# A four-layer encoder step on one core: score matrices of two heads issued in turn, and PSUM banks dealt out anew

## The chip, the core and the metric

The kernel runs on one core of a Trainium2 chip. That core has a matrix engine (TensorE, PE in the profile, with its weight loads as PEld), a vector engine (VectorE, DVE), an activation engine (ScalarE, ACT), a general engine (GpSimd, POOL) and a queue that issues DMAs (SP). Matrix results go to PSUM, which the kernel uses as eight banks of 128 partitions by 512 floats; everything else lies in SBUF. The metric is device time in microseconds (us) of one launch, the median of three runs.

## What is computed

One step of a streaming encoder: 512 prompt rows and 128 sample rows (8 groups of 16) of width 1024 go through two layers. Layer 0 has stick-breaking attention (8 heads of 64) beside a gated linear recurrence, layer 1 has chunk-band softmax attention (16 heads of 64); each layer ends in a gated feed-forward network of 2816. The sample rows also attend to 512 cached keys and values per group. Cut to what the change touches:

```python
def _sb_block(q, k, v, q_pos, k_pos):            # layer 0
    z = einsum('bthd,bshd->bhts', q, k) * HEAD_DIM ** -0.5
    mask = k_pos[None, :] < q_pos[:, None]
    log_beta = log_sigmoid(z)
    log_keep = where(mask, log_sigmoid(-z), 0.0)
    rev = cumsum(log_keep, axis=3, reverse=True)
    w = where(mask, exp(log_beta + after), 0.0)  # after: rev moved on by one
    return einsum('bhts,bshd->bthd', w, v)

def _band_attn(q, k, v, q_pos, k_pos, rel_table): # layer 1
    s = einsum('bthd,bshd->bhts', q, k) * HEAD_DIM ** -0.5
    s = s + rel_table[:, rel]
    p = softmax(where(mask, s, -inf))
    return einsum('bhts,bshd->bthd', p, v)
```

## The kernel before, in words

The program is a chain of stages: the stick-breaking layer (0 to 447 us of the profile), its feed-forward network, the chunk-band layer (about 885 to 1369 us), the second feed-forward network. Large products are made of two rounded halves of each operand, so that three matmuls stand for one.

**Prompt attention** (`attend_prompt`, L426) takes heads in pairs and, for each pair, four blocks of 128 query rows against n = 128, 256, 384 and 512 keys. A head has 64 channels, so head 0 of a pair lies in partitions 0 to 63 of `qT` and `kT` and head 1 in 64 to 127, and the three score matmuls of a head (L436, L437, L438) use 64 rows of the matrix engine. Before, one head's three matmuls are written together, its scores `z` become weights on the vector and activation engines (`stick_break` L400, `softmax` L413), the weights are transposed back into the same bank `z` (L444), copied out (L447 on ACT for head 0, L449 on DVE for head 1), and the result of both heads goes into the first head's bank (L455) and out at L457. So one bank is held from the first score to the end of its block.

**Sample attention** (`attend_sample`, L473) runs for each of 8 groups, once in the stick-breaking layer and twice (two halves of the heads) in the chunk-band layer, so 8 and 16 samples. A sample loads 1 MB of values (`vr`, L481) and four key tiles of 256 KB (`kr`, four buffers, L486). Each key tile is transposed on the matrix engine (`kttp`, L489), copied to SBUF (`kt`, two buffers: L494 on ACT, L492 on DVE) and gives a quarter of the scores (`zs`, L496). The scores are copied out (L499), become weights, are transposed (L508), copied (L509); the weights of the new keys are transposed (L510) and copied (L511); then come the products with the values (L517), a copy (L520), a last transpose (L521) and two copies to `oS` (L525). Before, all the PSUM results of a sample after the key tiles use the sample's score bank `zs`.

**PSUM.** Three banks (`pps`) serve the projections. The other five are two pools inside `mixer_pools`: before, 3 banks `za` and 2 banks `zb` in the stick-breaking layer, 4 and 1 in the chunk-band layer. `za` held scores; `zb` held the recurrence's results (`b_mix`), the transposed keys of the projections (`ktp`, L388) and key tiles. In the chunk-band layer (`KTC`) key tiles alternated between `zb` and `za`. Tiles of a pool take its banks in the order in which the program asks for them, so a tile that is asked for early and used late stands ahead of the later ones.

**What sets the order.** The program text gives each instruction a priority, and a scheduler of the framework fixes one order for each engine when the program is built; on the chip each engine works through its list in that order, and an instruction that waits holds up those behind it. Projections (`pw`, L288 to L290, and `pm`) and the output projection (`po`, L561 to L563) are the work that the scheduler puts between the steps of attention.

Of the kernel before, what the change touches and what calls it, by code (L numbers as in the profile page):

```python
# [16 lines left out]
P = 128  # L17
# [29 lines left out]
BANKS = ((3, 2), (4, 1))  # L47
KTA = "bbbb"
KTC = "baba"
# [6 lines left out]
def kernel(  # L56
# [8 lines left out]
    nc = tc.nc  # L65
# [360 lines left out]
    def attend_prompt(qT, kT, v, c0, odst, weights, mask):  # L426


        for b in range(4):
            n = (b + 1) * P  # L430
            bs = slice(b * P, n)
            wTs, zs = [], []
            for h in range(2):
                z = za([P, 512], "z")
                r = slice(64 * h, 64 * h + 64)
                MM(z[:, :n], lhsT=qT[r, 0, bs], rhs=kT[r, 0, :n], start=True, stop=False)  # L436
                MM(z[:, :n], lhsT=qT[r, 0, bs], rhs=kT[r, 1, :n], start=False, stop=False)  # L437
                MM(z[:, :n], lhsT=qT[r, 1, bs], rhs=kT[r, 0, :n], start=False, stop=not mask)  # L438
                if mask:
                    MM(z[:, bs], lhsT=identb, rhs=mask_a, start=False, stop=True)  # L440
                w = weights(h, n, z[:, :n])
                wT = vr_([P, b + 1, P], "wT")
                for j in range(b + 1):
                    nc.tensor.transpose(z[:, j * P:(j + 1) * P], w[:, j * P:(j + 1) * P], ident)  # L444
                zv = z[:, :n].rearrange("p (j t) -> p j t", t=P)
                if h == 0:
                    nc.scalar.copy(wT, zv)  # L447
                else:
                    nc.vector.tensor_copy(wT, zv)  # L449
                wTs.append(wT)  # L450
                zs.append(z)
            o = zs[0][:, :P]
# [20 lines left out]
    def attend_sample(ck, cv, b, cs, qbd, zn, vnew, weights, oS, kttp):  # L473
# [9 lines left out]
        for j in range(4):  # L483
# [3 lines left out]
            tp = (zb if kttp[j] == "b" else za)([P, 4, P], "kttp")  # L487
# [13 lines left out]
        w = weights(zs)  # L501
        wn = w5([P, DB, DS], "wn")
# [249 lines left out]
    stack.enter_context(mixer_pools(*BANKS[0]))  # L752
# [60 lines left out]
    def a_sample():  # L813
        with priority(FIRST + 100000):
            zn = new_key_scores(qbd, kfs, msn)
        for b in range(DB):
            with priority(FIRST + 100000 + 1000 * (b + 1)):
                attend_sample(cache_a_k, cache_a_v, b, slice(0, 512), qbd, zn, vt4[:, :512],
                              lambda zs: stick_break(528, zs, zs), oS[:, :4, :], KTA)
# [227 lines left out]

    stack.enter_context(mixer_pools(*BANKS[1]))
    W = w_qkv_c[0]
# [32 lines left out]
    def c_sample(half):  # L1082
# [11 lines left out]
        for b in range(DB):  # L1094
            with priority(p + 1000 * (b + 1)):
                attend_sample(cache_c_k, cache_c_v, b, cs, qbd[half], zn, vt4[:, cs],
                              lambda zs: softmax(528, zs, zs, bsam[:, ::-1]),
                              oS[:, 4 * half:4 * half + 4, :], KTC)
# [69 lines left out]
```

## Time and profile before

| | us |
|---|---|
| median of three runs (1822.29 to 1827.14) | 1823.97 |
| the profiled execution's own time | 1823.8 |
| its span in the trace | 1822.1 |
| TensorE busy (95% of the span) | 1732.9 |
| VectorE, ScalarE, GpSimd busy | 1142.8, 833.8, 327.7 |

In the page, a group of instructions has its line, its engine, its output and inputs by tile name, the shape and the count. Durations of matmuls run from the start of the read to a modelled end, so a matmul's duration is longer than the distance to the next one's start; where the argument is about throughput it uses distances of starts in the timeline. A matmul with f32 inputs stands as two in the trace, one with rounded inputs (the scores, projections) as one.

### The profile page before, as it was taken

The page shows a single profiled execution, that of the slowest core. Times are in us where ns is not written, and L with a number is a line of the kernel's source. Part 1 is how long each engine was busy: PE and PEld are TensorE (multiplying, and loading weights), DVE is VectorE, ACT ScalarE, POOL GpSimd, SP SyncE. Part 2 cuts the span into 40 slices and gives each one's busy share as a digit, 9 for nine tenths or more (in the row PEclk, how much of TensorE's full clock was granted, in tenths as well). Part 3 has the DMA queues.
Part 4 walks back from the last instruction along what each step waited for, and adds up shares of the span by engine and source line. Part 5 has one row for each costly group of instructions (what it writes and reads, how often), then busy time and mean ns, then how long its engine had stood idle before and what let it go on. Part 6 is the DMA issues. An engine that isn't in the chain of part 4 may idle for free.

```text
span 1822.1 us, 31879 instructions
## 1 busy us (share of the span) xinstructions
PE 1732.9 (95%) x12504; PEld 1550.1 (85%) x12504; DVE 1142.8 (63%) x2285; ACT 833.8 (46%) x1837; POOL 327.7 (18%) x355
## 2 busy tenths in 40 slices
PE   8999998998899999999799999999878999999997
PEld 7898986976898989989698888888757989999896
DVE  5466576767964846747635554665658747658475
ACT  6453444556642534525424333444545525435253
POOL 2000000002513413222200000000104314133130
PEclk9998997998999999999799999999988999999999
DMA  5311222573222232221342223257862222312212
GB/s 141 94 56 47 66 83 95 179 255 105 70 93 70 75 100 63 100 74 66 110 128 77 80 89 95 85 178 263 278 214 65 81 81 72 103 58 93 93 59 81
DMA packets 157430, 192.10 MB, mean 105 GB/s; under 512 B 13232, under 2 KB 109504, under 8 KB 157280
## 3 DMA queue, kind: packets, MB, share of 16 engines
q1 hardware_dynamic: 153696, 178.40, 30.4%
q0 software_dynamic: 3584, 11.67, 2.0%
q8 instruction: 98, 1.61, 0.4%
q14 instruction: 52, 0.43, 0.1%
HBM read 175.75 MB, written 14.29 MB: 104 GB/s over the span
## 4 chain that ended last, share of the span: by engine, by line
PE 80%; DVE 12%; DMA 4%; ACT 2%; issue 2%; SPq 0%; DVEq 0%; ACTq 0%
PE pn L307 6%; PE pn L309 5%; PE pn L308 5%; PE pw L288 5%; PE pw L289 5%; PE pw L290 5%; DVE wl L274 4%; PE px L653 3%; PE px L654 3%; PE px L655 3%; PE z L455 3%; PE py L655 3%; DMA kr<-in_cache_c_k_dram 2%; PE pm L337 2%; PE py L653 2%; PE py L654 2%
## 5 line engine op out<-in xcount | busy, mean ns | idle before, releaser
L274 DVE TENSOR_TENSOR wl<-raw,wh 128x512 fp32r<-128x512 f32 (+1 forms) x350 | 279.3, 807 | 220.8 <-ACT wh L273 218.7
L273 ACT CAST wh<-raw 128x512 fp32r<-128x512 f32 (+1 forms) x350 | 215.4, 618 | 347.3 <-PE pn L309 162.6
L659 POOL TENSOR_TENSOR sw<-raw 128x512 f32<-128x512 f32 x88 | 121.6, 1386 | 498.9 <-DMA raw<-in_w_ffn_gate_dram 292.9
L273 ACT CAST wh<-sw 128x512 fp32r<-128x512 f32 x176 | 109.3, 621 | 177.8 <-PE px L654 78.2
L274 DVE TENSOR_TENSOR wl<-sw,wh 128x512 fp32r<-128x512 f32 x176 | 139.7, 798 | 60.3 <-ACT wh L273 49.1
L308 PE MATMUL pn<-wl,gT 128*128 128x512 f32 x440 | 172.7, 393 | 0.0
L309 PE MATMUL pn<-wh,gT 128*128 128x512 f32 x440 | 170.7, 392 | 0.0
L307 PE MATMUL pn<-wh,gT 128*128 128x512 f32 x440 | 168.8, 394 | 0.0
L655 PE MATMUL py<-xb,wl 128*128 128x320 f32 x352 | 113.1, 321 | 8.4 <-DVE wl L274 8.2
L653 PE MATMUL py<-xb,wh 128*128 128x320 f32 x352 | 111.4, 316 | 6.1 <-ACT wh L273 4.6
L654 PE MATMUL pq<-xt,wh 128*128 128x320 f32 x352 | 109.1, 310 | 2.9 <-DVE xt L613 2.7
L654 PE MATMUL px<-xt,wh 128*128 128x320 f32 x352 | 109.7, 312 | 1.6 <-DVE xt L613 1.6
L654 PE MATMUL py<-xb,wh 128*128 128x320 f32 x352 | 110.7, 314 | 0.0
L653 PE MATMUL px<-xt,wh 128*128 128x320 f32 x352 | 109.5, 311 | 0.0
L655 PE MATMUL px<-xt,wl 128*128 128x320 f32 x352 | 109.4, 311 | 0.0
L653 PE MATMUL pq<-xt,wh 128*128 128x320 f32 x352 | 109.1, 310 | 0.1
L655 PE MATMUL pq<-xt,wl 128*128 128x320 f32 x352 | 108.6, 309 | 0.0
L309 PEld LDWEIGHTS pn<-wh,gT 128*128 128x128 f32 x440 | 83.5, 190 | 17.4
L308 PEld LDWEIGHTS pn<-wl,gT 128*128 128x128 f32 x440 | 83.6, 190 | 17.2
L307 PEld LDWEIGHTS pn<-wh,gT 128*128 128x128 f32 x440 | 83.4, 190 | 16.8
L288 PE MATMUL pw<-hTa,wh 128*128 128x320 f32 (+1 forms) x272 | 89.5, 329 | 0.0
L290 PE MATMUL pw<-hTa,wl 128*128 128x320 f32 (+1 forms) x272 | 88.7, 326 | 0.0
(331 smaller groups left out, 4778.3 us busy)
## 6 DMA issues: line engine op xcount, KB each, us to landing
raw<-in_w_ffn_gate_dram SPq DMA_DIRECT2D x44, 512.0 KB, 4.1
raw<-in_w_ffn_up_dram SPq DMA_DIRECT2D x44, 512.0 KB, 3.7
raw<-in_w_ffn_down_dram SPq DMA_DIRECT2D x44, 512.0 KB, 3.3
kr<-in_cache_c_k_dram SPq DMA_DIRECT2D x64, 256.0 KB, 4.8
vr<-in_cache_c_v_dram SPq DMA_DIRECT2D x16, 1024.0 KB, 6.7
raw<-in_w_in_ab_dram SPq DMA_DIRECT2D x24, 512.0 KB, 3.8
raw<-in_w_qkv_c_dram SPq DMA_DIRECT2D x24, 512.0 KB, 3.8
vr<-in_cache_a_v_dram SPq DMA_DIRECT2D x8, 1024.0 KB, 5.5
```

The lines of the kernel that those rows point to most:

```text
L273: nc.scalar.copy(H, rawv)
L274: nc.vector.tensor_sub(L, rawv, H.bitcast(F32))
L288: MM(ps[i], lhsT=H[:, k % 4, :], rhs=hT[k][:, 0, s], start=(k == 0), stop=False)
L289: MM(ps[i], lhsT=H[:, k % 4, :], rhs=hT[k][:, 1, s], start=False, stop=False)
L290: MM(ps[i], lhsT=L[:, k % 4, :], rhs=hT[k][:, 0, s], start=False, stop=(k == 7))
L307: MM(ps[b], lhsT=lhs[k][:, 0, bs], rhs=H, start=(k == 0), stop=False)
L308: MM(ps[b], lhsT=lhs[k][:, 0, bs], rhs=L, start=False, stop=False)
L309: MM(ps[b], lhsT=lhs[k][:, 1, bs], rhs=H, start=False, stop=(k == K - 1))
L653: MM(ps, lhsT=H[:, k, :], rhs=X[x][0][k], start=(first and k == 0), stop=False, **f)
L654: MM(ps, lhsT=H[:, k, :], rhs=X[x][1][k], start=False, stop=False, **f)
L655: MM(ps, lhsT=L[:, k, :], rhs=X[x][0][k], start=False, stop=(k == 3), **f)
L659: nc.gpsimd.tensor_tensor(t, a, b, op=op)
```

## The change

In `attend_prompt` both heads' score banks are asked for first, and the three score matmuls are written for head 0 and head 1 in turn. A score bank now ends with the weights: the transposes go to a tile `wtp` of `zb`, and the result into the first head's `wtp`. In `attend_sample` the score bank `zs` ends with the copy L499 (L502 after); all later PSUM results of the sample go to a new tile `zw` of `zb`, asked for after the weights. Every key tile is in `zb`. Both layers have 2 banks `za` and 3 banks `zb`; `ktp` and the recurrence share those three.

```diff
--- before.py
+++ after.py
@@ -44,9 +44,7 @@
 ORDER = "V0 P0 G0 P1 K0 V1 M0 P2 K1 R0 M1 R2 P3 R1 R3"
 MPRI = 50000
 WHEN = ((20, 20, 20, 20), (4, 8, 12, 15))
-BANKS = ((3, 2), (4, 1))
-KTA = "bbbb"
-KTC = "baba"
+BANKS = (2, 3)
 GROUPS = (6, 6, 6, 4)
 FIRST = -1000000
 LOGSET = "natural_log_exp_and_others"
@@ -426,30 +424,35 @@
     def attend_prompt(qT, kT, v, c0, odst, weights, mask):
 
 
+
         for b in range(4):
             n = (b + 1) * P
             bs = slice(b * P, n)
-            wTs, zs = [], []
-            for h in range(2):
-                z = za([P, 512], "z")
-                r = slice(64 * h, 64 * h + 64)
-                MM(z[:, :n], lhsT=qT[r, 0, bs], rhs=kT[r, 0, :n], start=True, stop=False)
-                MM(z[:, :n], lhsT=qT[r, 0, bs], rhs=kT[r, 1, :n], start=False, stop=False)
-                MM(z[:, :n], lhsT=qT[r, 1, bs], rhs=kT[r, 0, :n], start=False, stop=not mask)
-                if mask:
+            zs = [za([P, 512], "z") for _ in range(2)]
+
+            for i, j in ((0, 0), (0, 1), (1, 0)):
+                for h in range(2):
+                    r = slice(64 * h, 64 * h + 64)
+                    MM(zs[h][:, :n], lhsT=qT[r, i, bs], rhs=kT[r, j, :n], start=(i + j == 0),
+                       stop=(i == 1 and not mask))
+            if mask:
+                for z in zs:
                     MM(z[:, bs], lhsT=identb, rhs=mask_a, start=False, stop=True)
-                w = weights(h, n, z[:, :n])
+            ws_ = [weights(h, n, zs[h][:, :n]) for h in range(2)]
+            wTs, ts = [], []
+            for h, w in enumerate(ws_):
+                t = zb([P, 512], "wtp")
                 wT = vr_([P, b + 1, P], "wT")
                 for j in range(b + 1):
-                    nc.tensor.transpose(z[:, j * P:(j + 1) * P], w[:, j * P:(j + 1) * P], ident)
-                zv = z[:, :n].rearrange("p (j t) -> p j t", t=P)
+                    nc.tensor.transpose(t[:, j * P:(j + 1) * P], w[:, j * P:(j + 1) * P], ident)
+                tv = t[:, :n].rearrange("p (j t) -> p j t", t=P)
                 if h == 0:
-                    nc.scalar.copy(wT, zv)
+                    nc.scalar.copy(wT, tv)
                 else:
-                    nc.vector.tensor_copy(wT, zv)
+                    nc.vector.tensor_copy(wT, tv)
                 wTs.append(wT)
-                zs.append(z)
-            o = zs[0][:, :P]
+                ts.append(t)
+            o = ts[0][:, :P]
             for j in range(b + 1):
                 for h in range(2):
                     MM(o[64 * h:64 * h + 64, :], lhsT=v[:, j, c0 + 64 * h:c0 + 64 * h + 64],
@@ -470,7 +473,7 @@
             nc.vector.tensor_tensor(zn, zp, mask.unsqueeze(1).to_broadcast([P, DB, DS]), op=ALU.add)
         return zn
 
-    def attend_sample(ck, cv, b, cs, qbd, zn, vnew, weights, oS, kttp):
+    def attend_sample(ck, cv, b, cs, qbd, zn, vnew, weights, oS):
 
 
         def rows(src):
@@ -484,7 +487,7 @@
             kr = kr_([P, 512], "kr")
             with plain():
                 nc.sync.dma_start(kr, rows(ck)[:, j, :])
-            tp = (zb if kttp[j] == "b" else za)([P, 4, P], "kttp")
+            tp = zb([P, 4, P], "kttp")
             for p in range(4):
                 nc.tensor.transpose(tp[:, p, :], kr[:, p * P:(p + 1) * P], ident)
             kt = kt_([P, 4, P], "kt")
@@ -499,6 +502,7 @@
         nc.scalar.copy(zs[:, :512], z)
         nc.gpsimd.tensor_copy(zs[:, 512:], zn[:, b, :])
         w = weights(zs)
+        z = zb([P, 512], "zw")
         wn = w5([P, DB, DS], "wn")
         nc.gpsimd.memset(wn, 0.0)
         nc.gpsimd.tensor_copy(wn[:, b, :], w[:, 512:528])
@@ -749,7 +753,7 @@
 
 
     stack = ExitStack()
-    stack.enter_context(mixer_pools(*BANKS[0]))
+    stack.enter_context(mixer_pools(*BANKS))
     nc.scalar.preload_act_table_set(LOGSET)
     with priority(2 * FIRST):
         x0 = [load_x(x_rows(x_prompt, xs_flat, 0), 0)]
@@ -816,7 +820,7 @@
         for b in range(DB):
             with priority(FIRST + 100000 + 1000 * (b + 1)):
                 attend_sample(cache_a_k, cache_a_v, b, slice(0, 512), qbd, zn, vt4[:, :512],
-                              lambda zs: stick_break(528, zs, zs), oS[:, :4, :], KTA)
+                              lambda zs: stick_break(528, zs, zs), oS[:, :4, :])
 
 
     def b_gates():
@@ -1045,7 +1049,7 @@
     hT = hT2
 
 
-    stack.enter_context(mixer_pools(*BANKS[1]))
+    stack.enter_context(mixer_pools(*BANKS))
     W = w_qkv_c[0]
     vt4 = v4([P, D], "vt4c")
     vc = [vp([P, 4, 512], "vc") for _ in range(2)]
@@ -1095,7 +1099,7 @@
             with priority(p + 1000 * (b + 1)):
                 attend_sample(cache_c_k, cache_c_v, b, cs, qbd[half], zn, vt4[:, cs],
                               lambda zs: softmax(528, zs, zs, bsam[:, ::-1]),
-                              oS[:, 4 * half:4 * half + 4, :], KTC)
+                              oS[:, 4 * half:4 * half + 4, :])
 
     for half in range(2):
         p0 = 4 * half
```

The number of matmuls is the same. The order on the engines is not. Four places show it; names with numbers are tiles, and the lines of the new kernel are those of the text after the change (L436 is all three score matmuls, L447 the transposes, L458 the results; L492, L499, L512, L514, L521, L525 are L489, L496, L508, L510, L517, L521 of before).

On the matrix engine, chunk-band layer, second pair of heads, query block of 384 keys, before (`z_10370` is head 0's bank; head 1's follows 15 projection matmuls further on):

```order
L444 MATMUL z_10333<-ident_67,s_10337 128x128 x2
L288 MATMUL pw1_10559<-hTc2_9242,wh_10526 128x320
L289 MATMUL pw1_10559<-hTc2_9242,wh_10526 128x320
L455 MATMUL z_10300<-wT_10327,vc_9537 64x128
L436 MATMUL z_10370<-kTc_10151,qTc_10150 128x384
L437 MATMUL z_10370<-kTc_10151,qTc_10150 128x384
L438 MATMUL z_10370<-kTc_10151,qTc_10150 128x384
L290 MATMUL pw1_10559<-hTc2_9242,wl_10527 128x320
L288 MATMUL pw1_10559<-hTc3_9243,wh_10526 128x320
```

The same block after the change (`z_10422` is head 0's, `z_10423` head 1's):

```order
L286 MATMUL pw0_10590<-hTc4_9284,wh_10586 128x320
L436 MATMUL z_10422<-kTc_10199,qTc_10198 128x384 x2
L436 MATMUL z_10423<-kTc_10199,qTc_10198 128x384 x2
L458 MATMUL wtp_10372<-wT_10373,vc_9577 64x128
L436 MATMUL z_10422<-kTc_10199,qTc_10198 128x384
L436 MATMUL z_10423<-kTc_10199,qTc_10198 128x384
L287 MATMUL pw0_10590<-hTc4_9284,wh_10586 128x320
L288 MATMUL pw0_10590<-hTc4_9284,wl_10587 128x320
```

The heads stand beside each other, though not in strict turn: the scheduler has set two of one head, then two of the other. Over the whole program, a score matmul directly follows one of the other head 18 times before (5 in the stick-breaking layer, 13 in the chunk-band layer) and 88 times after (15 and 73: 42 at 128 keys, 31 at 256, 15 at 384, none at 512; before 7, 10, 1 and none). At 512 keys, and in most blocks of the stick-breaking layer, one head's three still follow each other.

On the matrix engine in the second half of the chunk-band layer's samples, before (`zs_13724`, `zs_13826`, `zs_13928`, `zs_14030` are four successive samples):

```order
L496 MATMUL zs_13928<-kt_13962,qbdc_9540 32x128 x4
L489 MATMUL kttp_13970<-ident_67,kr_13968 128x128 x4
L489 MATMUL kttp_14033<-ident_67,kr_14031 128x128 x4
L508 MATMUL zs_13826<-ident_67,zsb_13879 128x128 x4
L521 MATMUL zs_13724<-ident_67,osb_13819 128x128
L496 MATMUL zs_13928<-kt_13975,qbdc_9540 32x128 x4
L496 MATMUL zs_14030<-kt_14038,qbdc_9540 32x128 x4
L489 MATMUL kttp_14059<-ident_67,kr_14057 128x128 x4
L489 MATMUL kttp_14046<-ident_67,kr_14044 128x128 x4
L510 MATMUL zs_13826<-ident_67,wn_13889 128x128
L517 MATMUL zs_13826<-vr_13824,wTs_13892 32x128 x16
L517 MATMUL zs_13826<-vt4c_9536,wT4_13893 32x128 x4
```

The same place after (`zs_13735` and its later bank `zw_13798` are one sample, `zs_13838` is the next one):

```order
L499 MATMUL zs_13735<-kt_13782,qbdc_9580 32x128 x4
L512 MATMUL zw_13798<-ident_67,zsb_13788 128x128 x4
L492 MATMUL kttp_13841<-ident_67,kr_13839 128x128 x4
L492 MATMUL kttp_13854<-ident_67,kr_13852 128x128 x4
L514 MATMUL zw_13798<-ident_67,wn_13799 128x128
L499 MATMUL zs_13838<-kt_13846,qbdc_9580 32x128 x4
L492 MATMUL kttp_13867<-ident_67,kr_13865 128x128 x4
L521 MATMUL zw_13798<-vr_13733,wTs_13802 32x128 x16
L521 MATMUL zw_13798<-vt4c_9576,wT4_13803 32x128 x4
L499 MATMUL zs_13838<-kt_13859,qbdc_9580 32x128 x4
L499 MATMUL zs_13838<-kt_13872,qbdc_9580 32x128 x4
L492 MATMUL kttp_13880<-ident_67,kr_13878 128x128 x4
```

Before, the transposes of a sample's weights (L508 of `zs_13826`) stand behind most of the next sample's scores and the first key tile of the one after that. After, they stand directly behind the sample's own last scores, and the next sample's first key tile stands behind them. Of the fifteen steps from one sample's weights to the next in the chunk-band layer, the first four hold 71, 76, 6 and 48 `po` matmuls and the last eleven none. Between a sample's last scores and its weights' transposes stand 51, 48, 53, 0 and 14 of them for the first five samples and none for the other eleven. In the stick-breaking layer's eight samples 84, 99, 41 and 25 stand there for the first four and none for the last four.

On the activation engine at that place after (`zsb` is the sample's score copy, which turns into its weights; `wTs`, `wT4` are the transposed weights, `kt` key tiles):

```order
L502 COPY zsb_13891<-zs_13838 128x512
L419 ACTIVATE zsb_13891,tot_13895<-zsb_13891,m_13894 128x528
L513 COPY wTs_13905<-zw_13901 128x512
L497 COPY kt_13949<-kttp_13944 128x512
L515 COPY wT4_13906<-zw_13901 128x128
L497 COPY kt_13975<-kttp_13970 128x512
L502 COPY zsb_13994<-zs_13941 128x512
```

Here one sample's work follows the sample before it without any of it being moved ahead: score copy, exponential, transposed weights, then the next sample's key tiles and its score copy.

## Prediction

> **What bounds the kernel now.** The page first: the matrix engine (PE) is busy in almost the whole span.
>
> ```profile
> span 1822.1 us, 31879 instructions
> PE 1732.9 (95%) x12504; PEld 1550.1 (85%) x12504; DVE 1142.8 (63%) x2285; ACT 833.8 (46%) x1837; POOL 327.7 (18%) x355
> ```
>
> That is an average, so next the table of windows, cut at the stages that the change touches: prompt attention of the stick-breaking layer, its samples, prompt attention of the chunk-band layer, its samples. The columns are the stretch, its length, busy time with counts for PE, PEld, DVE, ACT and POOL, the granted clock, DMA share and GB/s.
>
> ```profile
> 63.00:307.00 244.00, 242.44 (x1661) 208.62 (x1659) 153.78 (x308) 116.50 (x268) 8.65 (x15) 0.95 0.21 62
> 307.00:447.00 140.00, 124.21 (x1337) 105.71 (x1336) 97.72 (x187) 79.61 (x168) 12.82 (x32) 0.92 0.57 191
> 954.00:1200.00 246.00, 246.00 (x1739) 207.16 (x1737) 137.58 (x458) 94.81 (x254) 13.43 (x26) 1.00 0.27 84
> 1200.00:1369.00 169.00, 146.27 (x1958) 119.76 (x1956) 96.19 (x260) 84.66 (x197) 14.69 (x52) 0.95 0.74 247
> ```
>
> Both prompt stretches have no idle PE to speak of (the third none in 246 us), with VectorE at 56 to 63%: there a shorter score phase shortens the kernel. Both sample stretches idle for 16 and 23 us, and the second moves 247 GB/s: there something else ends the waits. The rest of the span is feed-forward work that the change leaves alone.
>
> **Scores in turn: the gain.** The timeline of the chunk-band layer, PE rows (start, duration, line, shape, count). First one head alone at 512 keys, then the one place where two heads happen to stand beside each other, then two output-projection matmuls.
>
> ```profile
> 1198.21 0.50 PE L436 MATMUL z<-kTc,qTc 64*128 64x512 f32 x1
> 1198.54 0.39 PE L437 MATMUL z<-kTc,qTc 64*128 64x512 f32 x1
> 1198.78 0.39 PE L438 MATMUL z<-kTc,qTc 64*128 64x512 f32 x1
> 1199.10 0.55 PE L444 MATMUL z<-ident,s 128*128 128x128 f32 x3
> ```
>
> ```profile
> 955.37 0.33 PE L437 MATMUL z<-kTc,qTc 64*128 64x128 f32 x2
> 955.54 0.28 PE L438 MATMUL z<-kTc,qTc 64*128 64x128 f32 x2
> 955.65 0.34 PE L437 MATMUL z<-kTc,qTc 64*128 64x256 f32 x2
> 955.82 0.29 PE L438 MATMUL z<-kTc,qTc 64*128 64x256 f32 x2
> ```
>
> ```profile
> 1195.99 0.28 PE L562 MATMUL po<-wl,oHL 128*128 128x256 f32 x1
> 1196.11 0.28 PE L563 MATMUL po<-wh,oHL 128*128 128x256 f32 x1
> ```
>
> A lone head's matmuls start 0.33, 0.24 and 0.32 us apart at 512 keys. In the pairs, the two matmuls at 955.54, one of each head, together span 0.28 us, which is what a single matmul of 128 columns takes from start to end (0.27 us in the row at 1333.99 below): the second starts with the first and is free. A step to the other head is therefore worth one start distance: 0.17 and 0.11 us at 128 keys (955.37 to 955.54 to 955.65; I take 0.14), 0.17 at 256 (955.65 to 955.82), 0.22 at 384 (between 256 and 512, an estimate).
>
> What counts is how many such steps the built order has: 35 more at 128 keys, 21 more at 256, 14 more at 384, none at 512. So 35 x 0.14 + 21 x 0.17 + 14 x 0.22 = 4.9 + 3.6 + 3.1 = 11.6 us, of which 10 steps, 1.4 us, lie in the stick-breaking layer. The first of three lone matmuls holds the array 0.09 us longer than the second (0.33 against 0.24), and a score run is left and entered some 20 times less, worth 2 us. **Together 13.5 us**: 12 in the chunk-band layer, where PE is the bound and all of it should show, and 1.5 in the other. The bounds are 10 and, if steps were in full turn everywhere, 32 us: a lone head costs 0.89 us at 512 keys (1198.21 to 1199.10), by estimate from the distances above 0.7, 0.55 and 0.5 at the smaller ones, and one of each pair's two would vanish, 12 x 2.65.
>
> The Trainium skill's page "TensorEngine Tiling (Array Packing)", in its table "Theoretical Speedup", promises up to twice the rate where the contracted dimension is 64 or less. By that rule the term would be the 32 us and the sum 1851; the pairs above agree with it, but a pair has to stand beside each other in the order, and most do not.
>
> Score banks fall from 3 and 4 to 2, but are given back once the scores are read, before transposes and results. Between blocks stand 15 to 25 projection matmuls in the chunk-band layer, so I cost that at nothing there. In the stick-breaking layer the transposes now wait in `zb` behind the recurrence's tiles; the projections cover it for the most part: 0, with bounds of 8 us either way. If the cover is gone, the last two pairs' blocks wait for a chain of weights of about 5 us each, twice.
>
> **Samples: the loss.** Before, one sample's weights are worked out while PE has the next sample's key tiles. This is that chain in the timeline where little else disturbs it, first the PE rows from one sample's last scores (1332.47) to its transposes (1336.95), with the next samples' work between:
>
> ```profile
> 1332.47 0.67 PE L496 MATMUL zs<-kt,qbdc 128*32 128x128 f32 x16
> 1333.07 1.09 PE L489 MATMUL kttp<-ident,kr 128*128 128x128 f32 x8
> 1333.99 0.27 PE L510 MATMUL zs<-ident,wn 128*128 128x128 f32 x1
> 1334.62 1.08 PE L517 MATMUL zs<-vr,wTs 128*32 128x128 f32 x32 [0.35 <-ACT wT L511]
> 1335.52 0.40 PE L517 MATMUL zs<-vt4c,wT 128*32 128x128 f32 x8
> 1335.74 0.62 PE L496 MATMUL zs<-kt,qbdc 128*32 128x128 f32 x16
> 1336.29 0.66 PE L489 MATMUL kttp<-ident,kr 128*128 128x128 f32 x4
> 1336.95 0.33 PE L508 MATMUL zs<-ident,zsb 128*128 128x128 f32 x1
> ```
>
> Then ACT and DVE over the same time:
>
> ```profile
> 1332.36 0.59 ACT L509 COPY wTs<-zs 128x512 f32<-128x512 f32 x1 [0.21 <-PE zs L508]
> 1332.99 0.59 ACT L499 COPY zsb<-zs 128x512 f32<-128x512 f32 x1
> 1333.81 0.59 ACT L494 COPY kt<-kttp 128x512 f32<-128x512 f32 x1 [0.23 <-PE kttp L489]
> 1334.30 0.27 ACT L511 COPY wT<-zs 128x128 f32<-128x128 f32 x1
> 1335.34 0.74 ACT L421 ACTIVATE zsb<-zsb,m 128x528 f32<-128x528 f32 x1 [0.77 <-DVE m L420]
> 1335.98 0.19 ACT L421 ACTIVATION_READ_ACCUMULATOR zsb<-zsb,m 128x1 f32 x1
> ```
>
> ```profile
> 1333.72 0.71 DVE L418 CUSTOM_DVE_ANT_0 zsb<-zsb,bsam 128x528 f32<-128x528 f32 x1 [0.69 <-ACT zsb L499]
> 1334.36 0.08 DVE L418 DVE_READ_ACCUMULATOR2_ANT m<- 128x1 f32 x1
> 1334.47 0.69 DVE L492 COPY kt<-kttp 128x512 f32<-128x512 f32 x1
> 1335.08 0.14 DVE L420 TENSOR_SCALAR m<-m 128x1 f32<-128x1 f32 x1
> 1336.20 0.16 DVE L422 RECIPROCAL tot<-tot 128x1 f32<-128x1 f32 x1 [0.98 <-ACT zsb L421]
> 1336.40 0.49 DVE L423 TENSOR_SCALAR zsb<-zsb,tot 128x528 f32<-128x528 f32 x1
> ```
>
> The chain is 0.59 + 0.71 + 0.08 + 0.14 + 0.74 + 0.19 + 0.16 + 0.49 = 3.1 us and some 0.1 us at each of its hand-overs, so about 4.0; here it was 3.96 from the start of the score copy to the transposes (1332.99 to 1336.95), with one key-tile copy in between. After the change the transposes stand on PE directly behind the sample's last scores. PE takes its list in order, so it waits these 4.0 us, and behind it wait the next sample's key-tile transposes, and with them its copies on ACT and DVE, its scores, and the key buffers that SP reloads. Then comes the way to the next last scores. Four transposes 0.66, copy L509 0.59 and, behind it on ACT, the first key-tile copy 0.59, with hand-overs: 2.0 us. Then on PE the first quarter of scores 0.28, the third key tile 0.46 (half of 1333.07 to 1333.99), the products 1.12 (1334.62 to 1335.74) and two quarters 0.55 (to 1336.29): 2.4 us. Then the fourth key tile 0.66, its copy 0.69 and the last quarter, with hand-overs: 1.8 us. That is 6.2 us, and **one sample takes 10.2 us** where nothing else stands between.
>
> What a sample took before, from the one new-key transpose (L510) per sample of the chunk-band layer, with first and last start:
>
> ```profile
> L510 PE MATMUL zs<-ident,wn x16: 272/273/447, 1220.1 to 1348.2; 128*128 128x128 f32 x16
> ```
>
> Fifteen steps in 128.1 us are 8.5 each, output projection included. After, the last eleven steps hold none of that: 11 x 10.2 = 112. A `po` matmul takes 0.12 us (1195.99 to 1196.11). In the first four steps 48, 53, 0 and 14 of them cover the wait of 4.0 us and the others lie beside the shorter waits or add a little: 6.2 + 48 x 0.12 + 1 = 13.0, likewise 13.6, then 10.2, and with 34 outside the wait 12.2. Sum 161, so **33 us more**. The attention tail has no key tiles left to fill it before the first sample: 4 us more. The DMAs do not bind, since 2 MB in 10 us are 200 GB/s and the stretch had 247. Bounds for the two: 15 us, if the wait is half hidden, and 48.
>
> In the stick-breaking layer the chain has a scan. Its first step after the copy, and the transposes that wait for it:
>
> ```profile
> 402.04 0.67 ACT L403 ACTIVATE l<-zsb 128x528 f32<-128x528 f32 x1
> ```
>
> ```profile
> 408.44 0.90 PE L508 MATMUL zs<-ident,zsb 128*128 128x128 f32 x3 [2.86 <-ACT zsb L411]
> ```
>
> That is 6.4 us, and 0.6 for the copy before it; I take off 0.5 for other work on DVE, so 6.5. The `po` matmuls between last scores and transposes cover 84 x 0.12, 99 x 0.12, 4.9 and 3.0 us, then nothing. Idle: 0, 0, 1.6, 2.6 and 5.6 (eight other transposes in each of these two), and three times 6.5, in all 29 us. The waits that go are at most the 16 us of idle time in this stretch, of which half lies at its end in work that stays. **I take 17 us more**, between 10 and 29.
>
> Low clock is the last term. The row with one DMA wait of 3 us (columns as above):
>
> ```profile
> 1329.53 1.94 PE L489 MATMUL kttp<-ident,kr 128*128 128x128 f32 x8 [3.08 <-DMA kr<-in_cache_c_k_dram]
> ```
>
> Eight transposes took 1.94 us after it, against 1.09 at 1333.07: after 3 us of rest PE ran at little more than half its rate. New rests of 4.0 us some twelve times and of about 6 four times, each with perhaps 0.4 us of slower work on the chain, give **6 us**, between 0 and 35 (2.2 us of PE work more in each of sixteen steps, if all of it ran at half rate).
>
> **Sum.** Against the profiled execution's 1823.8 us (its span 1822.1 and 1.7 around it; the three runs' median is 1823.97): -13.5 + 33 + 4 + 17 + 6 = +46.5, so **1870 us**.
>
> **Rivals.**
> *The wait only takes the place of a DMA wait, and the score gain stays.* For it: in the row above PE waited 3.08 us for a key tile, and 8.5 us a sample at 247 GB/s is near what the DMAs give; the new loads run under the weights. Against it: 10.2 us is a chain without any DMA in it. It decides if a bare sample takes under 7.8 us; then the samples cost nothing more and the time is 1824 - 13.5 = 1810, faster.
> *Half.* The chain is shorter by hand-overs, or PE's rests of before go too: samples +15 to 20, stick-breaking +5 to 10, no clock term: 1830 to 1840.
> *Clock.* PE stays slow through all samples: 35 instead of 6, which makes 1899. The Trainium skill's page "TensorE: Matmul & The Clock Gate", section "Why this matters for your kernels", says to leave no rest over about 3 us between bursts, or the clock falls to half. Of its two cases the row at 1329.53 agrees; rests of 4.0 us repeated eleven times are in no trace yet.
> *The shared banks bind.* Recurrence and transposes in the same three banks hold up the stick-breaking layer: 8 to 20 us more, 1878 to 1890.
>
> **Numbers.** Forecast with its bounds, 1840 to 1895, 0.66; between faster and half 0.02; the shared banks 0.05; clock 0.08; half 0.10; faster 0.09. The range 1834 to 1895 leaves out the faster case, the clock case and the low end of half. About 0.3% is what a measurement of this kernel can tell from no change: faster 0.09; within it 0.04, what lies between the faster case and half and a little of half; slower 0.87.
>
> **What the profile would show.** Right: L436 rows in pairs at equal starts; the stretch 954 to 1200 some 12 us shorter; L514 rows 10 us apart towards the end of the samples; PE idle before L512 waiting for `zsb` from L421 (about 45 us in all) and L409 (about 25). Wrong: L512 with little idle time before it, or key tiles waiting for DMAs as before; then the samples' term falls. A longer stick-breaking prompt stretch would show the shared banks.

## The result and the profile after

Over four runs each the changed kernel took 1923.35 us (1920.16 to 1928.69) and the kernel before, on the same chip, 1823.13 us (1821.09 to 1827.14). The ratio is 1.0568, with a 95% interval of 1.0541 to 1.0595: 100 us slower, where 46.5 were forecast and 1895 us was the upper end of the range. The profiled execution took 1928.69 us, its span is 1926.6.

The page of the changed kernel, in the rows shown of before. PE's busy time has risen by 26 us with the same 12504 matmuls, and the span by 104.5:

```profile
span 1926.6 us, 31982 instructions
PE 1758.7 (91%) x12504; PEld 1565.3 (81%) x12504; DVE 1151.6 (60%) x2285; ACT 832.9 (43%) x1837; POOL 328.7 (17%) x355
```

The table of windows, cut at the same places of the program (stick-breaking prompt, its samples, chunk-band prompt, its samples; columns as in the prediction):

```profile
63.00:325.00 262.00, 253.44 (x1682) 214.75 (x1681) 161.95 (x322) 115.27 (x272) 9.93 (x17) 0.91 0.21 62
325.00:497.00 172.00, 127.78 (x1331) 107.39 (x1331) 92.66 (x175) 81.53 (x169) 12.85 (x31) 0.86 0.46 149
1007.00:1241.00 234.00, 232.70 (x1644) 196.60 (x1644) 132.44 (x448) 89.69 (x249) 12.99 (x25) 1.00 0.28 85
1241.00:1473.00 232.00, 172.40 (x2049) 140.15 (x2049) 103.01 (x271) 91.25 (x205) 16.91 (x55) 0.85 0.55 182
```

The reader compares lengths first: +18, +32, -12 and +63 us, together 101, so the change's own stages hold nearly all of the loss. Then idle time, which is length less PE's busy time. In the last stage it went from 22.7 to 59.6 us (+36.9), in the second from 15.8 to 44.2 (+28.4), in the first from 1.6 to 8.6 (+7.0). What is left is busy time: +26.1 in the last stage, of which the 91 further matmuls, moved there from the stage before, are only a small part. The granted clock fell there from 0.95 to 0.85, in the second stage from 0.92 to 0.86 and in the first from 0.95 to 0.91.

What PE waited for, first in the stick-breaking samples (325 to 497), then in the chunk-band ones (1241 to 1473); the columns are total time, count and longest:

```profile
PE zw L512 <- ACT zsb L409: 27.0, 5, 8.7
```

```profile
PE zw L512 <- DVE zsb L421: 43.8, 12, 5.7
PE zs L499 <- DVE kt L495: 6.3, 10, 0.7
...
PE zw L512 <- DVE rv L224: 1.7, 1, 1.7
```

Those are the waits for a sample's weights in front of its transposes. The waits for key tiles from the DMAs, which the timeline of before showed, are no longer among the first. One chunk-band sample on PE, from the transposes of its weights to the next ones:

```profile
1399.38 1.09 PE L512 MATMUL zw<-ident,zsb 128*128 128x128 f32 x4 [3.51 <-DVE zsb L421]
1400.26 1.91 PE L492 MATMUL kttp<-ident,kr 128*128 128x128 f32 x8
1401.97 0.42 PE L514 MATMUL zw<-ident,wn 128*128 128x128 f32 x1
1402.32 0.65 PE L499 MATMUL zs<-kt,qbdc 128*32 128x128 f32 x8
1402.90 1.11 PE L492 MATMUL kttp<-ident,kr 128*128 128x128 f32 x4
1403.95 1.65 PE L521 MATMUL zw<-vr,wTs 128*32 128x128 f32 x32
1405.43 0.39 PE L521 MATMUL zw<-vt4c,wT 128*32 128x128 f32 x8
1405.64 0.61 PE L499 MATMUL zs<-kt,qbdc 128*32 128x128 f32 x16
1406.19 0.66 PE L492 MATMUL kttp<-ident,kr 128*128 128x128 f32 x4
1406.68 0.27 PE L525 MATMUL zw<-ident,osb 128*128 128x128 f32 x1
1407.63 0.43 PE L499 MATMUL zs<-kt,qbdc 128*32 128x128 f32 x8 [0.67 <-DVE kt L495]
```

The wait of 3.51 us was forecast at 4.0. After it the eight transposes take 1.91 us (1.09 in the timeline of before) and the 32 products 1.65 (1.08), while the 16 scores at 1405.64 run at the old 0.61: the array is slow for some 6 us after the wait, then fast, then waits again. The slow part is not always so long. In the next step, after a wait of 3.52 us, the eight transposes are slow again, but the products are back at 1.08 us:

```profile
1412.05 1.92 PE L492 MATMUL kttp<-ident,kr 128*128 128x128 f32 x8
1415.61 1.08 PE L521 MATMUL zw<-vr,wTs 128*32 128x128 f32 x32
```

The scores now stand in pairs at 128 and 256 keys and in part at 384, but not at 512, where three of one head still stand alone:

```profile
1011.51 0.62 PE L436 MATMUL z<-kTc,qTc 64*128 64x256 f32 x6
...
1021.58 0.96 PE L436 MATMUL z<-kTc,qTc 64*128 64x512 f32 x3
```

### The profile page after: what moved, and what is told of

The parts are those of the page before. It is cut to its first block, busy times and chain, and to the rows that moved or that the text cites. A ratio compares the mean times of both kernels' runs of the same rounds, so it can differ in the third digit from the quotient of the medians.

```text
span 1926.6 us, 31982 instructions
## 1 busy us (share of the span) xinstructions
PE 1758.7 (91%) x12504; PEld 1565.3 (81%) x12504; DVE 1151.6 (60%) x2285; ACT 832.9 (43%) x1837; POOL 328.7 (17%) x355
## 4 chain that ended last, share of the span: by engine, by line
PE 79%; DVE 14%; ACT 3%; issue 2%; DMA 1%; SPq 0%; DVEq 0%; ACTq 0%
PE pn L305 5%; PE pn L307 5%; PE pn L306 5%; PE pw L287 4%; PE pw L286 4%; PE pw L288 4%; DVE wl L272 4%; PE px L657 3%; PE px L658 3%; PE px L659 3%; PE kttp L492 3%; PE z L436 3%; PE wtp L458 2%; PE py L659 2%; PE pm L337 2%
## 5 line engine op out<-in xcount | busy, mean ns | idle before, releaser
L272 DVE TENSOR_TENSOR wl<-raw,wh 128x512 fp32r<-128x512 f32 (+1 forms) x350 | 284.4, 822 | 231.9 <-ACT wh L271 229.6
L305 PEld LDWEIGHTS pn<-wh,gT 128*128 128x128 f32 x440 | 83.3, 190 | 16.8
L286 PE MATMUL pw<-hTa,wh 128*128 128x320 f32 (+1 forms) x272 | 88.9, 327 | 1.2 <-DVE qT L364 1.2
L287 PE MATMUL pw<-hTa,wh 128*128 128x320 f32 (+1 forms) x272 | 88.2, 324 | 0.0
```

The costliest lines, as they stand in the source:

```text
L272: nc.vector.tensor_sub(L, rawv, H.bitcast(F32))
L286: MM(ps[i], lhsT=H[:, k % 4, :], rhs=hT[k][:, 0, s], start=(k == 0), stop=False)
L287: MM(ps[i], lhsT=H[:, k % 4, :], rhs=hT[k][:, 1, s], start=False, stop=False)
L305: MM(ps[b], lhsT=lhs[k][:, 0, bs], rhs=H, start=(k == 0), stop=False)
```

## The experiments

Theory after the result: (1) `zw` is asked for before the next sample's key tiles, so PE has nothing to do during each sample's weights; (2) these rests put the clock down, and the slow array makes each step longer than its chain; (3) in the stick-breaking layer transposes and recurrence take turns in the three banks. Rivals: too few score banks are what slows the samples; the long steps have other causes than the clock; the pairs themselves hold the stick-breaking layer up.

Lengths of the stages, in us, worked out from the starts of marks in each trace: prompt attention from first to last score (SB: stick-breaking, CB: chunk-band), tail to the first sample's weights transposes, samples from the first to the last weights transpose; in between and at the end the feed-forward parts.

| run | SB prompt | tail | samples | between | CB prompt | tail | samples | end |
|---|---|---|---|---|---|---|---|---|
| before | 240.6 | 38.8 | 72.7 | 535.5 | 245.6 | 16.4 | 130.4 | 475.1 |
| changed | 256.9 | 30.0 | 113.7 | 537.8 | 234.4 | 20.3 | 189.4 | 475.5 |
| zs_kept | 250.8 | 32.7 | 93.2 | 534.3 | 234.4 | 20.2 | 139.4 | 470.1 |
| c_only | 239.4 | 38.7 | 73.0 | 535.1 | 234.4 | 20.2 | 139.2 | 469.3 |
| scores_first | 255.2 | 31.6 | 74.5 | 538.4 | 234.4 | 25.5 | 132.1 | 471.9 |
| fill | 259.2 | 30.0 | 108.0 | 533.5 | 234.4 | 20.3 | 173.1 | 469.6 |
| pairs_only | 242.6 | 38.6 | 72.6 | 533.7 | 246.0 | 16.8 | 133.2 | 470.0 |
| c_four | 240.5 | 38.9 | 72.7 | 533.7 | 233.0 | 17.5 | 130.9 | 475.5 |
| c_turns | 241.0 | 38.2 | 72.7 | 538.4 | 235.5 | 19.9 | 128.5 | 472.0 |
| c_mirror | 241.2 | 38.1 | 72.4 | 533.4 | 234.4 | 18.9 | 127.0 | 476.2 |
| mirror_turns | 243.9 | 38.7 | 72.7 | 535.8 | 236.4 | 20.1 | 130.1 | 477.0 |
| a_three | 243.1 | 33.8 | 76.1 | 536.2 | 234.4 | 18.9 | 127.7 | 474.4 |

The two feed-forward columns scatter by 5 and 8 us whatever was edited; so much of a single profile is chance.

**No bank asked for after the weights (zs_kept).**

```diff
         w = weights(zs)
-        z = zb([P, 512], "zw")
```

> The changed kernel, but a sample's transposed weights and results go back into the bank that held its scores; no bank `zw` is asked for after the weights. Prompt attention is untouched. Theory (PE stands still for each sample's weights because `zw` is asked for ahead of the next sample's key tiles): the chunk-band sample steps fall from 188.7 us (first to last sample's weights transposes) to about 135, the stick-breaking ones from 113.0 to about 80, and the time from 1923 to 1830 to 1850; what is then left over 1823 is the 16 us of the stick-breaking prompt stretch less the 11 of the chunk-band one. Rival (two score banks instead of three and four are what slows the samples): both stretches stay within 15 us of the changed kernel, 1895 to 1920.

It took 1847.37 us, 1.0166 of the kernel before (1.0140 to 1.0191). One line gives 73 us back (1.0568 less 1.0166, of 1820). The chunk-band steps are near the forecast (139.4 against about 135), the stick-breaking ones are longer (93.2 against about 80). A likely reason is that with two score banks kept through, in place of three, the next sample starts later; c_mirror, below, bears it out for the chunk-band layer, and for the other it was not tried. The windows of its two sample stages:

```profile
319.00:473.00 154.00, 125.45 (x1333) 103.46 (x1333) 91.67 (x177) 80.80 (x169) 12.27 (x31) 0.90 0.50 167
1214.00:1395.00 181.00, 153.91 (x2050) 120.04 (x2049) 102.54 (x270) 88.41 (x205) 17.07 (x55) 0.97 0.70 234
```

In the second, PE runs at 0.97 again and idles for 27 us, not 60. The first rival is wrong in its main point; what remains of the longer samples may be its.

**The next sample's scores asked for first (scores_first).** The function stops before `zw`, and its caller runs the next sample's first half before this one's second half.

```diff
         w = weights(zs)
+        yield
         z = zb([P, 512], "zw")
...
+        for p, g in samples:
+            with priority(p):
+                next(g)
+            late.append((p, g))
+            if len(late) > 1:
+                finish(*late.pop(0))
+        finish(*late.pop(0))
```

> The changed kernel with all its banks and `zw`, but the code asks for the next sample's key tiles and scores before it asks for this sample's `zw`. Theory (the order in which tiles are asked for from the shared three banks fixes what PE may do during the weights): PE has the next sample's key tiles during the weights, the chunk-band steps fall from 188.7 us to 130 to 150, the stick-breaking ones from 113 to 80 to 95, and the time is 1840 to 1870. Rival (three banks for key tiles, transposes and results are too few whatever the order): steps within 10 us of the changed kernel, 1900 or more.

It took 1835.24 us, 1.0107 of before (1.0076 to 1.0137), better than the 1840 to 1870 forecast: with every bank and `zw` itself as in the changed kernel, the samples are at 74.5 and 132.1 us, within 2 us of before. It is the place of the request in the code, not the number of banks, that kept PE waiting. In the window of the chunk-band samples the DMAs move 236 GB/s again, against 182:

```profile
1203.00:1382.00 179.00, 154.91 (x2051) 119.56 (x2050) 103.20 (x270) 86.93 (x205) 17.55 (x55) 0.98 0.70 236
```

**Idle PE given something to do (fill).**

```diff
         nc.scalar.copy(zs[:, :512], z)
+        for _ in range(fill):
+            MM(z, lhsT=identb, rhs=rst[:, :512], start=True, stop=True)
```

> The changed kernel with matmuls that serve nothing put into the wait: once a sample's scores are copied, 14 bf16 matmuls of 128x512 (chunk-band, from the sixth sample on) or 26 (stick-breaking, from the fifth on) write over its score bank, about 3 and 5.7 us of PE work at 0.22 us each, in waits of 3.5 and 6.5 us. Nothing that is computed changes. Theory (the way after each wait is long, 7.5 to 8 us where 6.2 were forecast, because the clock falls to half in the wait): the granted clock stays near 1, the bare chunk-band step falls from 11.5 us to about 10.2, and the time falls by 12 to 25 us, to 1898 to 1911. Rival (the way is long for other reasons: copies, hand-overs, key tiles that arrive late): the steps stay at 11.5 and the time within 5 us of 1923, or rises by what of the filling runs over the waits.

It took 1900.88 us, 1.0456 of before (1.0438 to 1.0473). Against the changed kernel's 1.0568 that is 1.1% of 1820, or 20 us faster with 258 matmuls more (4 x 26 and 11 x 14) that serve nothing. A step of its trace, to be read beside that of the changed kernel:

```profile
1401.14 0.60 PE L514 MATMUL zw<-ident,zsb 128*128 128x128 f32 x4
1401.58 1.04 PE L492 MATMUL kttp<-ident,kr 128*128 128x128 f32 x8
...
1403.84 1.08 PE L523 MATMUL zw<-vr,wTs 128*32 128x128 f32 x32
...
1406.95 0.43 PE L499 MATMUL zs<-kt,qbdc 128*32 128x128 f32 x8 [0.67 <-DVE kt L495]
1408.08 3.18 PE L504 MATMUL zs<-rst,identb 128*128 128x512 bf16 x13 [0.70 <-ACT zsb L502]
1411.10 0.60 PE L514 MATMUL zw<-ident,zsb 128*128 128x128 f32 x4
```

The L504 row is the filling (13 of its 14 matmuls are in the trace). The eight transposes take 1.04 us and the products 1.08; from the transposes of one sample (1401.14) to those of the next (1411.10) are 9.96 us. The new-key transposes of the sixteen chunk-band samples, in both kernels, from first to last start (187.2 and 170.7 us):

```profile
L514 PEld LDWEIGHTS zw<-ident,wn x16: 138/230/231, 1265.1 to 1452.3; 128*128 128x128 f32 x16
```

```profile
L516 PEld LDWEIGHTS zw<-ident,wn x16: 138/139/230, 1257.5 to 1428.2; 128*128 128x128 f32 x16
```

The window of the same stage in it, with the clock at 0.97 in place of 0.85:

```profile
1234.00:1449.00 215.00, 185.62 (x2197) 138.48 (x2207) 105.03 (x270) 90.59 (x205) 17.61 (x55) 0.97 0.58 197
```

So filling gave back 16.5 us of the chunk-band loss and 5.7 of the stick-breaking one (113.7 to 108.0), and in its rows that is the array's rate after the waits. The first samples of each stage were left unfilled, so the slow array cost at least that much. Theory (2) holds.

**The stick-breaking layer as before (c_only)** has the old prompt attention and samples there, with 3 and 2 banks, and in the chunk-band layer the new prompt attention with `zs` kept:

```diff
-BANKS = (2, 3)
+BANKS = ((3, 2), (2, 3))
+KTA = "bbbb"
+KTC = "bbbb"
```

> The stick-breaking layer wholly as before (3 and 2 banks, its PE order the same row by row); in the chunk-band layer the new prompt attention with 2 and 3 banks, while samples keep their score bank. Theory (the 16 us more of the stick-breaking prompt stretch come from transposes and recurrence taking turns in the three banks): that stretch is back at 240.6 us against 256.9, the chunk-band prompt stretch keeps its gain of 11 us, and the time is 1808 to 1825, faster than before or equal. Rival (the 16 us are a low clock that would come anyway, or the two score banks cost the chunk-band samples as much as the pairs give): over 1825.

It took 1816.92 us, 0.9984 of before (0.9965 to 1.0002): no difference that is sure. The stick-breaking stretch is back (239.4), the chunk-band prompt stretch keeps its 234.4, but the samples take 139.2 against 130.4.

**Pairs in turn and nothing else (pairs_only).** The six score matmuls of a block in the changed order, in the kernel before.

```diff
-                MM(z[:, :n], lhsT=qT[r, 0, bs], rhs=kT[r, 0, :n], start=True, stop=False)
...
+            for i, j in ((0, 0), (0, 1), (1, 0)):
+                for h in range(2):
+                    r = slice(64 * h, 64 * h + 64)
+                    MM(zs[h][:, :n], lhsT=qT[r, i, bs], rhs=kT[r, j, :n], start=(i + j == 0),
```

> The kernel before with one part of the change: the scores of a pair's heads are written in turn; transposes and results stay in the score banks, the banks stay 3 and 2, then 4 and 1, samples as before. In the order 39 score steps go to the other head (18 before, 88 in the changed kernel), 12 of 14 new or old ones in the stick-breaking layer at 128 keys as in the changed kernel. Theory (the stick-breaking prompt stretch grew by 16 us through the shared three banks, not through the pairs): that stretch is 238 to 242 us; the chunk-band one gains only 2 to 4 us of its 245.6; the time is 0.997 to 1.000 of the kernel before. Rival (the pairs, which need two score banks at once, hold the stick-breaking blocks up): that stretch 250 us or more, 1.005 or more.

It took 1820.62 us, 1.0004 of before (0.9983 to 1.0026). The stick-breaking stretch is 242.6 us, so the pairs don't hold it up. The chunk-band stretch gained nothing (246.0), a miss by 2 to 4 us: with 25 steps to the other head in this layer, 13 before, too little changes to be seen.

**Transposes out of the shared banks (a_three).** On top of c_mirror, below:

```diff
-                t = zb([P, 512], "wtp")
+                t = (za if mask else zb)([P, 512], "wtp")
```

> The same kernel without the ties, and in the stick-breaking layer the changed prompt attention too, but with its transposes and results in the three score banks, so that the recurrence has its two banks for itself. Samples there as before. Theory (the 16 us that this stretch grew by come from the three banks shared with the recurrence): the stretch is 238 to 244 us, not 256.9, and the time 0.993 to 0.998 of the kernel before. Rival (weights of both heads before either's transposes, or the order of the pair, hold up this layer whose PE has little other work): the stretch is 249 us or more, and the time 0.998 to 1.004.

It took 1810.73 us, 0.9942 of before (0.9919 to 0.9964). The stretch is 243.1 us, with new code and new pairs, when the recurrence has its own two banks, and 256.9 when transposes stand in line with it, although the attention has fewer banks here (three in all) than in the changed kernel (two, and a share of three). Theory (3) holds for the stretch. What the shared banks cost in the end is less, since in the changed kernel the tail behind the stretch is shorter; this is worked out below.

**Which banks let the pairs pay.** Four kernels keep the stick-breaking layer of before and vary the chunk-band layer. c_mirror gives samples one of the three banks and key tiles the two; c_four takes scores and transposes from four banks in rotation; c_turns and mirror_turns tie each score matmul of a pair behind the one before.

```diff
-        z = za([P, 512], "zs")
+        z = zz([P, 512], "zs")
```

```diff
-                t = zb([P, 512], "wtp")
+                t = za([P, 512], "wtp")
```

```diff
+                    with tc.issue_after(last.ins) if last else nullcontext():
+                        last = MM(zs[h][:, :n], lhsT=qT[r, i, bs], rhs=kT[r, j, :n], start=(i + j == 0),
+                                  stop=(i == 1 and not mask))
```

> The stick-breaking layer as before, the chunk-band layer with the changed kernel's prompt attention and its 2 and 3 banks; a sample's scores, transposes and results lie in one of the three banks, and the key tiles in the two. Theory (with two score banks kept through, only one sample can run ahead, which cost the chunk-band samples 8.8 us over before, 139.2 against 130.4): with three the samples fall to 128 to 134 us, the 11 us of the prompt stretch stay, 0.993 to 0.997 of the kernel before. Rival (the key tiles in two banks bind instead): samples at 138 or more, 0.998 or above.

> The stick-breaking layer as before; in the chunk-band layer the pairs with all four score banks in rotation, scores and transposes alike (4 and 1 banks), samples as before. The order has 122 steps to the other head in the chunk-band layer, 39 of them at 512 keys, where the changed kernel has 73 and none. Theory (two matmuls of different heads that stand beside each other run together, so a step is worth a start distance: 0.14 us at 128 keys, 0.17 at 256, 0.22 at 384, about 0.27 at 512; of five steps in a block three count): 39 pairs more or less in full, some 24 blocks times 3 matmuls saved, that is 8 x 3 x 0.27 + 8 x 3 x 0.22 + 8 x 3 x 0.14 + 3 x 0.17 = 15.6 us off the 245.6, samples back at 130.4, and 0.990 to 0.994 of the kernel before. Rival (at 512 keys two heads together are no faster than one after the other, since the array takes 512 columns either way): 4 to 8 us off, 0.996 to 0.999.

> As the kernel with four score banks in rotation, and each score matmul of a pair is tied behind the one before it, so that the built order has nearly all of them in turn: 146 steps in the chunk-band layer. Theory: 2 to 4 us less than with four banks in rotation alone, 0.988 to 0.993 of the kernel before. Rival (a tie makes a free head wait for the other's bank, and PE has nothing in between): 2 us or more slower than four banks alone.

> The kernel with the changed prompt attention in the chunk-band layer and the sample's bank among the three (key tiles in the two), and each score matmul tied behind the one before it in the pair: 117 steps to the other head in that layer instead of 73, 25 of them at 512 keys instead of none. With four banks in rotation 122 steps took PE's time on scores from 34.9 to 25.8 us. Theory (a step saves PE time, and with transposes in other banks nothing waits for it): score time 27 to 29 us, the prompt stretch 227 to 231 us against 234.4, 0.988 to 0.993 of the kernel before. Rival (with two score banks a tied head waits for the bank of the other, whose weights are still being read): the stretch stays at 233 to 238 us and the time at 0.993 to 0.998.

c_mirror took 1808.38 us, 0.9939 of before (0.9914 to 0.9964), its samples 127.0: the 8.8 us that c_only lost there came from two score banks kept through. c_four took 1808.12 us, 0.9928 (0.9904 to 0.9952). Both beat both kernels. In c_four most heads stand in turn at 128, 384 and 512 keys, but hardly any at 256 (4 matmuls start with a neighbour there, out of 24 that could, against 23 or 24 at each other size). At 512 keys, and the waits further on:

```profile
1165.11 0.96 PE L438 MATMUL z<-kTc,qTc 64*128 64x512 f32 x6
```

```profile
PE wtp L449 <- DVE tot L422: 3.9, 2, 2.1
PE wtp L449 <- DVE s L423: 1.6, 1, 1.6
```

Six matmuls of two heads take 0.96 us from first start to last end, as long as three of one head took before (1198.21 to 1198.78 and 0.39 more). By the distance from each score matmul's start to the next matmul's, summed over the stretch, the scores take 25.3 us, against 41.2 before and 34.6 in the changed kernel: 15.9 us less, where three saved of five steps gave 15.6. That rival, no gain at 512 keys, is wrong. But the stretch is only 12.6 us shorter: PE, which had no idle time in it before, now idles for 4.9 us (233.0 us less 228.1 busy), most of it in the waits for weights above, which stand at its end and, for 1.1 us, just behind it. The ties are no gain: c_turns took 1814.10 us, 0.9960 (0.9942 to 0.9978), mirror_turns 1813.95 us, 0.9953 (0.9934 to 0.9972); the stretch is 235.5 and 236.4 us, as their rivals said. In mirror_turns the scores take 33.4 us by the same count, where 27 to 29 were forecast (34.6 without the ties).

## Why the prediction was wrong

**Right: the mechanism and the idle time.** The wait for the weights was forecast at about 45 us in the chunk-band samples and 25 in the others; it is 45.5 (43.8 and 1.7 that ends at another VectorE row) and 27.0. PE's idle time in the chunk-band samples rose by 36.9 us, where 33 for the steps and 4 for the tail were summed. That these agree is in part luck, since the 33 were a length and not idle time: with the waits filled the steps still took 42.6 us more than before (170.7 less 128.1). The bare step of 10.2 us is 9.96 where the clock is whole.

**Failed: the clock term, "6 us, between 0 and 35".** The row at 1329.53 showed the slow array after a rest of 3 us, and the 2.2 us a step that it can cost stood in the bounds; I took 0.4 us a step as a guess. The last seven bare steps of the changed kernel (without its very last step) take 10.9 to 12.0 us, 11.5 in the mean, 1.5 above the filled ones. Filling part of the waits gave back 20 us by the medians and 22 by the two sample stages, where 6 were taken. The Trainium skill's page "TensorE: Matmul & The Clock Gate", section "Why this matters for your kernels", asks for no rest over about 3 us; rests of 3.5 us, repeated, agree with it here, and so do the filled rests, of 0.7 us, at a clock of 0.97 (its window above). The rival that was given 0.08 (35 us) was in good part true, beside the forecast and not in its place.

**Failed: the shared banks at "0, with bounds of 8 us either way".** The stick-breaking prompt stretch grew by 16.3 us (18 by the window, 7.0 of it idle and 11.0 busy). I had looked at the projections as cover for the transposes, and not at the line that transposes and recurrence form in the three banks. Not all of the growth is loss: the tail behind the stretch is 8.8 us shorter, as some projections moved from it into the stretch and many key tiles and scores of the samples into the stage behind. Up to the first sample's transposes the layer lost 7.5 us, and 4.1 to 9.8 in the three other kernels with these shared banks (zs_kept, scores_first, fill); in scores_first, whose samples take what they took before, the whole layer lost 9.2 (361.3 against 352.1). So the term is about 8 us, at its bound, and this rival (0.05, 8 to 20 us) was true at its low end. In the last 35 us of the stretch the clock is 0.56:

```profile
290.00:325.00 35.00, 30.26 (x119) 22.54 (x119) 23.49 (x42) 13.99 (x34) 1.30 (x2) 0.56 0.23 74
```

No single wait from 275 to 326 us is over 1.8 us, so the clock was low here without a rest of 3 us. By itself this low clock does not make the stretch longer: in a_three, whose stretch is 243.1 us, it was low for about as long near the end, and in fill, with 259.2, it was 0.82 over the last 38 us. The window of a_three:

```profile
289.60:320.30 30.70, 28.12 (x164) 21.35 (x164) 21.25 (x38) 12.01 (x25) 1.51 (x3) 0.50 0.39 123
```

Why the clock stayed low for so long was not tried and stays open.

**Failed: the stick-breaking samples at 17 us, "between 10 and 29".** Idle time in their window rose by 28.4. Of the 29 us of new waits I took 12 off for old ones that would go; the new ones came to 27.0, and about as much idle time as before stands beside them. From first to last weights transpose these samples take 41.0 us more, since to the waits come slower work (clock 0.85, 0.95 before) and key tiles and scores that the tail had before.

**Failed in its parts: the early and the last steps.** With the waits filled from the sixth sample on (fill) the chunk-band steps took 170.7 us against 161. The first four were 52.6 where 49 was worked out, the last 15.8 where 10.2 was: in it output matmuls of the sample rows stood ahead of the last scores and transposes.

**Right in sum, wrong inside: the pairs.** The chunk-band stretch is 11.1 us shorter, where 12 were forecast, and its tail 3.9 longer, where 4 were. But the scores themselves gained 6.6 us (41.2 to 34.6): about 3.5 us of the rest is work (64 new-key scores, 8 key-tile transposes, some transposes and products of the last blocks) that moved past the end of the stretch, into that tail. I counted a start distance for each of 60 more steps; in a run of turns only every second step is free, and 44 more matmuls start with their neighbour (57 against 13). The "Theoretical Speedup" table of the Trainium skill's "TensorEngine Tiling (Array Packing)" gives up to twice the rate; where the order allowed it (c_four) scores ran 41.2 / 25.3 = 1.6 times as fast, and the price of 32 us for both layers was right in kind: 15.9 in one layer.

**The range.** Forecast and rivals were set against each other as if one excluded the rest. Clock, banks and waits are separate terms, and each came out above what was taken. By the table of stages, the stick-breaking prompt and its tail are 9 us over the forecast (7.5 for -1.5), its samples 24 (41.0 for 17, at least 5.7 of it the clock), the chunk-band samples 26 (59.0 for 33: 16.5 the clock, 9 the early and last steps), the prompt before them with its tail 1. Less the 6 us that the forecast had for the clock these are 54, and 1824 + 46.5 + 54 is 1924, where 1923 was measured. Had the upper bounds of the terms been added (-10 + 48 + 29 + 35 + 8 = 110), the range would have reached 1934.

## What to carry to other kernels

Where tiles of a pool are handed out in the order of the code, a new tile asked for late in one pass of a loop stands ahead of the first tiles of the next pass: look for what it keeps the bottleneck engine from doing, before counting banks. When a wait on PE is longer than the rest after which the trace already shows slow matmuls, price the work behind it at the slow rate in every pass, not as a small extra. And unless two mechanisms truly exclude each other, add their bounds for the range instead of sharing out chances among them.

## What was not expected of the hardware

PE got faster by being given more to do: with 258 matmuls added that serve nothing the kernel took 20 us less. After a rest of 3.5 us the slow rate held for some 6 us of work in the step shown (transposes 1.91 us for eight, in place of 1.04), even though the array was busy nearly all that time; in the next step it held for some 3 us. And two 64-row matmuls with 512 columns ran side by side at no cost that the trace shows: six in the 0.96 us of three.
